# Both triangles of attention keys in one square of 128 columns, with masked values and their differences

## The chip, the cores and the metric

One core of one Trainium2 chip runs the whole program in one launch. The metric is the device time of an execution in microseconds. A core has TensorE (PE; its weight loads appear as PEld), VectorE (DVE), ScalarE (ACT), GpSimd (POOL) and SyncE (SP), each with a queue of its own that is worked off in order; they wait for one another by semaphores. SBUF is the on-chip memory, PSUM the memory of eight banks that TensorE writes to.

## The reference, cut to what matters

A decoder of two layers over 512 tokens of width 1024. Layer 0 is a gated token mixer, layer 1 sliding-window attention over shared keys and values; both have a gated feed-forward part and a gated per-layer embedding. The change lies in the attention of layer 1:

```
def mixer_b(xn, w_q, sinks, w_o, kblk, vblk):
    q = (xn @ w_q).reshape(B, nb, BLOCK, N_KV_HEADS, GQA_GROUP, HEAD_DIM)
    scores = einsum('bnikgd,bnjkd->bnkgij', q, kblk) * (HEAD_DIM ** -0.5)
    i = arange(BLOCK)[:, None];  j = arange(2 * BLOCK)[None, :]
    dist = i + BLOCK - j
    in_band = (dist >= 0) & (dist < WINDOW)
    valid = in_band[None] & ((blk > 0) | (j[None] >= BLOCK))
    scores = scores - slopes * dist
    scores = where(valid, scores, -inf)
    m = maximum(max(scores, axis=-1), sink)
    e = exp(scores - m)
    probs = e / (sum(e, axis=-1) + exp(sink - m))
    out = einsum('bnkgij,bnjkd->bnikgd', probs, vblk)
    return out.reshape(B, S, N_Q_HEADS * HEAD_DIM) @ w_o
```

BLOCK and WINDOW are 128, there are 4 blocks of queries, 16 query heads and 4 key heads; `kblk` and `vblk` hold the previous block and the own one, 256 keys. Of these, a query i of a block sees the own keys j up to i and the previous block's keys j above i: two triangles that together have 128 keys for each query.

## The kernel before

Activations lie with features on the partitions and the 512 tokens along the free dimension. Nearly every matmul operand is split into a high and a low part of type fp32r, and a product is three matmuls: high by high, high by low, low by high (`mm3`, lines 182 to 184; `mm3t`, 193 to 195, with tokens on the output's partitions). Weights come by DMA into a raw tile, ScalarE casts the high part (`wh`, line 155), VectorE subtracts it for the low part (`wl`, line 156), and `pump`, `chunk` and `more` set how far ahead this runs.

Attention goes in 16 steps, four groups (a key head with its four query heads) by four blocks of queries. A step has four functions. `scores(i)`: for each of the four heads two matmuls (lines 702, 703) of the queries with 256 keys (128 in the first block of a group, which has no previous block) into half a PSUM bank; then one VectorE operation (line 705) that adds the table `far` of distances (a huge negative outside the band), scales, takes the minimum with the sink and leaves the row's minimum in `neg`; then ScalarE's exponential with the row's sum in `sm` (line 710), and the sink's own exponential (713, 714). `weights(i)`: sum, reciprocal (720, 721) and the scaling of the four heads, two on VectorE (727), two on ScalarE (725). `turn(i)`: for each block of keys four TensorE transposes of 128x128 into a bank (737) and the split of that bank into a high and a low part by ScalarE and VectorE (240, 241). `mix(i)`: for each block of keys and each pair of heads three matmuls of the values with these (760), then the split of the result into `o2` (766, 767).

The loop over the steps emits `scores(i)`, then what the table `beside` gives for the step (projections of the next group's queries, two of the four value projections `values(c)`, pieces of the output projection `merge`), then `mix(i-2)`, `turn(i-1)` and `weights(i)`. Scores, turn and weights are marked as of high priority, so that the scheduler moves them ahead of the fill on each engine's queue. `values(0)` and `values(1)` are emitted before the loop, `values(2)` and `values(3)` in steps 2 and 3. The queries of a later group pass through `queries` (a scaled copy, a split, four DMAs). Tiles are drawn from pools by tag: `m0` to `m5` (1024 columns), the arena `ah0` to `al8` (512 columns), the two-buffer tags of the pool `tp`. The keys' normalized input `xkv` lies in the arena's slots 0 to 7, which the attention output `o2` takes over.

Of the kernel before, what the change touches and what calls it, by code (L numbers as in the profile page):

```python
# [8 lines left out]
F32 = mybir.dt.float32  # L9
F32R = mybir.dt.float32r  # L10
AF = mybir.ActivationFunctionType
ALU = mybir.AluOpType

P = 128
D = 1024
S = 512
KD = D // P
NC = S // P
# [3 lines left out]
SLOTS = 9  # L22
N = S // 2
HEADS = 16
HD = 64
GROUPS = 4
GQ = HEADS // GROUPS
EPS = 1e-6
FAR = 1e37
# [19 lines left out]
def tile_yoco(ctx: ExitStack, tc: tile.TileContext, t, out: bass.AP, out_b: bass.AP):  # L49
    nc = tc.nc  # L50

    const = ctx.enter_context(tc.tile_pool(name="const", bufs=1))
    hp = ctx.enter_context(tc.tile_pool(name="hp", bufs=1))
    xp = ctx.enter_context(tc.tile_pool(name="xp", bufs=1))
    ap = ctx.enter_context(tc.tile_pool(name="arena", bufs=1))
# [5 lines left out]
    def psum(name):  # L61
        return mmp.tile([P, S], F32, tag="mm", name=name)
# [161 lines left out]
    ps = psum("idle")  # L224
# [14 lines left out]
    def split(src, hi, lo):  # L239
        nc.scalar.copy(hi, src)  # L240
        nc.vector.tensor_sub(lo, src, hi.bitcast(F32))
# [71 lines left out]
    def slope(hd):  # L313
        return 2.0 ** (-8.0 * (hd + 1) / HEADS)
# [145 lines left out]
    for c in range(NC):  # L460
        vps[1].append(psum(f"v1_{c}"))
        mm3t(vps[1][c], xs, parts, 0, S, c)
        if c == 0:
            rt = n0.begin()


    far = const.tile([P, 2 * P], F32, name="far")
    nc.gpsimd.iota(far, pattern=[[1, 2 * P]], base=-P, channel_multiplier=-1,
                   allow_small_or_imprecise_dtypes=True)
    nc.gpsimd.affine_select(out=far, in_=far, pattern=[[-1, 2 * P]], compare_op=ALU.is_ge,  # L470
                            fill=-FAR, base=P, channel_multiplier=1)
    nc.gpsimd.affine_select(out=far, in_=far, pattern=[[1, 2 * P]], compare_op=ALU.is_ge,
                            fill=-FAR, base=-1, channel_multiplier=-1)

    qscale = const.tile([P, KD], F32, name="qscale")
    for hd in range(HEADS):
# [143 lines left out]
        nc.gpsimd.memset(x[:, VW - HD :].bitcast(F32), 0.0)  # L620


    box = {}

    def values(c):
        if c == 0:
            box["v"] = chunk(256, KD)
        ps = psum(f"vv{c}")
        mm3t(ps[:, :256], xkv, box["v"], 0, 256, c)
        pg = ps[:, :256].rearrange("p (g d) -> p g d", g=GROUPS)  # L630
        vh, vl = (x[:, : VW - HD].rearrange("p (c g w) -> p c g w", c=NC, g=GROUPS)[:, c, :, HD:] for x in vt)
        nc.scalar.activation(vh, pg, AF.Copy, scale=rt[:, c : c + 1])
        nc.vector.scalar_tensor_tensor(vl, pg, rt[:, c : c + 1], vh.bitcast(F32),
                                       op0=ALU.mult, op1=ALU.subtract)

    def project(g, j, k0, k1):
        if j == 0 and k0 == 0:
# [17 lines left out]
    def more():  # L655

        pump(state["unit"] + 1)

    beside = {
        -1: [(values, 0), (values, 1)],  # L660
        0: [(project, 1, 0, 0, 8), (more,)],
        1: [(project, 1, 1, 0, 8), (more,)],
        2: [(values, 2), (project, 2, 0, 0, 4)],
        3: [(values, 3), (project, 2, 0, 4, 8), (more,)],
        4: [(project, 2, 1, 0, 4), (more,)],
        5: [(project, 2, 1, 4, 8)],
        6: [(project, 3, 0, 0, 4), (more,)],
# [17 lines left out]
    steps = [(g, n) for g in range(GROUPS) for n in range(NC)]  # L685
    live = {}

    def scores(i):


        g, n = steps[i]
        k0 = 0 if n else P
        nk = 2 * P - k0
        t0 = (n - 1) * P + k0
        pr = mp.tile([P, GQ, 2 * P], F32, tag=f"m{4 + i % 2}", name=f"pr{i}")
        neg = at.tile([P, GQ], F32, tag="neg", bufs=2, name=f"neg{i}")
        for e in range(GQ):
            if e % 2 == 0:
                sc = psum(f"sc{i}_{e}")
            o = sc[:, (e % 2) * 256 : (e % 2) * 256 + nk]  # L700
            q = qs[g][e][:, n * P : (n + 1) * P]
            nc.tensor.matmul(o, q, kh[g // 2][:, g % 2, t0 : t0 + nk], start=True, stop=False)
            nc.tensor.matmul(o, q, kl[g // 2][:, g % 2, t0 : t0 + nk], start=False, stop=True)
            hd = GQ * g + e
            nc.vector.tensor_tensor_reduce(out=pr[:, e, :nk], in0=far[:, k0:], in1=o, scale=-slope(hd),
                                           scalar=nsink[:, hd : hd + 1], op0=ALU.add, op1=ALU.min,
                                           accum_out=neg[:, e : e + 1])
        sm = at.tile([P, GQ], F32, tag="sm", bufs=2, name=f"sm{i}")
        for e in range(GQ):
            nc.scalar.activation(pr[:, e, :nk], pr[:, e, :nk], AF.Exp, bias=neg[:, e : e + 1], scale=-1.0,  # L710
                                 accum_out=sm[:, e : e + 1])
        ds = at.tile([P, GQ], F32, tag="ds", bufs=2, name=f"ds{i}")
        nc.vector.tensor_add(ds, sink[:, GQ * g : GQ * (g + 1)], neg)
        nc.scalar.activation(ds, ds, AF.Exp)
        live[i] = (pr, nk, sm, ds)

    def weights(i):

        pr, nk, sm, ds = live[i]
        nc.vector.tensor_add(ds, ds, sm)  # L720
        nc.vector.reciprocal(ds, ds)
        for e in range(GQ):
            a, r = pr[:, e, :nk], ds[:, e : e + 1]
            if e in (1, 3):
                nc.scalar.activation(a, a, AF.Copy, scale=r)
            else:
                nc.vector.tensor_scalar_mul(a, a, r)
        live[i] = (pr, nk)

    def turn(i):  # L730

        pr, nk = live[i]
        pts = []
        for b in range(nk // P):
            tr = psum(f"tr{i}_{b}")
            for e in range(GQ):
                nc.tensor.transpose(tr[:, e * P : (e + 1) * P], pr[:, e, b * P : (b + 1) * P], ident)
            q = state["pt"] = (state["pt"] + 1) % 3
            if q == 2:
                ph, pl = (ap.tile([P, S], F32R, tag=f"a{x}{SLOTS - 1}", name=f"p{x}{i}_{b}") for x in "hl")  # L740
            else:
                ph, pl = pts4[:, 2 * q, :], pts4[:, 2 * q + 1, :]
            split(tr, ph, pl)
            pts.append((ph, pl))
        live[i] = pts

    def mix(i):
        g, n = steps[i]
        pts = live.pop(i)
        ps = psum(f"pv{i}")[:, : 2 * P]  # L750
        first = True
        for b, halves in enumerate(pts):
            c = n - len(pts) + 1 + b
            ph, pl = (a.rearrange("p (b e t) -> p b e t", b=2, e=2) for a in halves)
            for e in range(2):
                at0 = (c * GROUPS + g) * 2 * HD + (HD if e == 0 else 0)
                vh, vl = (x[:, at0 : at0 + P] for x in vt)
                for lhs, rhs in ((vh, ph), (vh, pl), (vl, ph)):
                    end = b == len(pts) - 1 and e == 1 and lhs is vl
                    nc.tensor.matmul(ps, lhs, rhs[:, :, e, :], start=first, stop=end)  # L760
                    first = False
        cols = slice(n * P, (n + 1) * P)
        for b in range(2):
            oh, ol = o2[2 * g + b]
            src = ps[:, b * P : (b + 1) * P]
            nc.scalar.copy(oh[:, cols], src)
            nc.vector.tensor_sub(ol[:, cols], src, oh[:, cols].bitcast(F32))
# [217 lines left out]
```

## Time and profile before

| | |
|---|---|
| three runs, median (lowest to highest) | 1160.1 us (1159.73 to 1160.7) |
| the profiled execution, its time | 1160.26 us |
| the profiled execution, its span | 1158.2 us |
| TensorE busy | 1145.4 us, 5464 matmuls |
| VectorE busy | 742.0 us |
| ScalarE busy | 529.0 us |
| GpSimd busy | 78.9 us |

The span reaches from the first instruction to the last. Busy time is the time in which at least one instruction of the engine is under way; matmuls overlap, so that a busy TensorE need not be at its best rate. A group of instructions is shown as line, engine, operation, output<-inputs by the program's names, the shapes, the count, then the busy time in us and the mean ns of one, then the idle time of the engine just before them with what ended it. A line in order of time begins with its start and its duration in us.

### The profile page before, as it was taken

The page shows a single profiled execution, that of the slowest core. Times are in us where ns is not written, and L with a number is a line of the kernel's source. Part 1 is how long each engine was busy: PE and PEld are TensorE (multiplying, and loading weights), DVE is VectorE, ACT ScalarE, POOL GpSimd, SP SyncE. Part 2 cuts the span into 40 slices and gives each one's busy share as a digit, 9 for nine tenths or more (in the row PEclk, how much of TensorE's full clock was granted, in tenths as well). Part 3 has the DMA queues.
Part 4 walks back from the last instruction along what each step waited for, and adds up shares of the span by engine and source line. Part 5 has one row for each costly group of instructions (what it writes and reads, how often), then busy time and mean ns, then how long its engine had stood idle before and what let it go on. Part 6 is the DMA issues. An engine that isn't in the chain of part 4 may idle for free.

```text
span 1158.2 us, 13843 instructions
## 1 busy us (share of the span) xinstructions
PE 1145.4 (99%) x5464; PEld 961.9 (83%) x5464; DVE 742.0 (64%) x1165; ACT 529.0 (46%) x860; POOL 78.9 (7%) x87
## 2 busy tenths in 40 slices
PE   9999999999999999999999999999999999999997
PEld 7888888888888888888888888888888888888896
DVE  7356467763676367556877886677636773675665
ACT  6534344431344234544667885544413432344542
POOL 2000310000000000032200002100000000000222
PEclk9999999999999999999999999999999999999999
DMA  9322322323323323233133314232232233224302
GB/s 318 117 82 73 109 76 106 109 73 109 109 64 100 109 91 109 91 109 104 42 92 110 87 43 170 85 109 85 98 109 82 91 100 109 91 88 150 109 1 73
DMA packets 30736, 115.42 MB, mean 100 GB/s; under 512 B 3016, under 2 KB 14928, under 8 KB 21200
## 3 DMA queue, kind: packets, MB, share of 16 engines
q1 hardware_dynamic: 29552, 113.37, 29.1%
q10 hardware_dynamic: 1120, 1.18, 0.3%
q8 instruction: 43, 0.70, 0.3%
q14 instruction: 21, 0.17, 0.0%
HBM read 108.24 MB, written 2.11 MB: 95 GB/s over the span
## 4 chain that ended last, share of the span: by engine, by line
PE 95%; DVE 2%; ACT 1%; issue 1%; DMA 1%; POOL 0%; SPq 0%; POOLq 0%; ACTq 0%
PE up L182 14%; PE up L184 14%; PE up L183 14%; PE d L184 8%; PE d L182 8%; PE d L183 8%; PE gate L182 2%; PE gate L184 2%; PE gate L183 2%; PE pv L760 1%; PE u L182 1%; PE u L183 1%; PE u L184 1%; PE o L182 1%; PE o L183 1%; PE o L184 1%
## 5 line engine op out<-in xcount | busy, mean ns | idle before, releaser
L156 DVE TENSOR_TENSOR wl<-wraw,wh 128x1024 fp32r<-128x1024 f32 (+2 forms) x197 | 239.4, 1216 | 133.5 <-ACT wh L155 132.9
L155 ACT CAST wh<-wraw 128x1024 fp32r<-128x1024 f32 (+1 forms) x196 | 202.1, 1033 | 265.8 <-PE d L183 131.6
L182 PE MATMUL up<-nf00h,wh 128*128 128x512 f32 x352 | 137.2, 390 | 0.0
L182 PE MATMUL up<-nf10h,wh 128*128 128x512 f32 x352 | 137.1, 389 | 0.0
L184 PE MATMUL up<-nf00h,wl 128*128 128x512 f32 x352 | 137.0, 389 | 0.0
L184 PE MATMUL up<-nf10h,wl 128*128 128x512 f32 x352 | 137.0, 389 | 0.0
L183 PE MATMUL up<-nf00l,wh 128*128 128x512 f32 x352 | 136.9, 389 | 0.0
L183 PE MATMUL up<-nf10l,wh 128*128 128x512 f32 x352 | 136.9, 389 | 0.0
L182 PE MATMUL d<-ah,wh 128*128 128x512 f32 x352 | 136.9, 389 | 0.0
L183 PE MATMUL d<-al,wh 128*128 128x512 f32 x352 | 136.9, 389 | 0.0
L184 PE MATMUL d<-ah,wl 128*128 128x512 f32 x352 | 136.9, 389 | 0.0
L351 ACT ACTIVATE c<-hs,vec 128x512 f32<-128x512 f32 x88 | 71.5, 815 | 71.7 <-DVE hs L347 71.1
L352 DVE SCALAR_TENSOR_TENSOR c<-hs,vec,c 128x511 f32<-128x511 f32 x88 | 65.8, 749 | 34.5 <-ACT c L351 34.5
L327 DVE TENSOR_TENSOR h<-h,d 128x512 f32<-128x512 f32 x56 | 38.4, 686 | 73.8 <-PE d L184 73.8
L184 PEld LDWEIGHTS up<-nf00h,wl 128*128 128x128 f32 x352 | 66.1, 188 | 13.9
L183 PEld LDWEIGHTS up<-nf10l,wh 128*128 128x128 f32 x352 | 66.1, 188 | 13.8
L184 PEld LDWEIGHTS up<-nf10h,wl 128*128 128x128 f32 x352 | 66.1, 188 | 13.8
L183 PEld LDWEIGHTS d<-al,wh 128*128 128x128 f32 x352 | 66.1, 188 | 13.8
L240 ACT CAST ah<-a 128x512 fp32r<-128x512 f32 x44 | 27.4, 622 | 109.7 <-DVE a L357 109.6
L184 PEld LDWEIGHTS d<-ah,wl 128*128 128x128 f32 x352 | 66.1, 188 | 13.7
L183 PEld LDWEIGHTS up<-nf00l,wh 128*128 128x128 f32 x352 | 66.1, 188 | 13.6
L182 PEld LDWEIGHTS d<-ah,wh 128*128 128x128 f32 x352 | 66.1, 188 | 13.7
(337 smaller groups left out, 2089.0 us busy)
## 6 DMA issues: line engine op xcount, KB each, us to landing
wraw<-in_w_up SPq DMA_DIRECT2D x44, 1024.0 KB, 4.8
wraw<-in_w_down SPq DMA_DIRECT2D x16, 896.0 KB, 4.6
wraw<-in_w_down SPq DMA_DIRECT2D x8, 1024.0 KB, 4.8
wraw<-in_w_u SPq DMA_DIRECT2D x4, 1024.0 KB, 5.4
wraw<-in_w_out SPq DMA_DIRECT2D x4, 1024.0 KB, 4.8
wraw<-in_w_gate SPq DMA_DIRECT2D x4, 1024.0 KB, 4.8
wraw<-in_w_q SPq DMA_DIRECT2D x4, 1024.0 KB, 5.2
wraw<-in_w_o SPq DMA_DIRECT2D x4, 1024.0 KB, 5.1
```

The lines of the kernel that those rows point to most:

```text
L155: nc.scalar.copy(wh[:, :n], src)
L156: nc.vector.tensor_sub(wl[:, :n], src, wh[:, :n].bitcast(F32))
L182: nc.tensor.matmul(ps, wh[:, a:b], xh, start=st, stop=False)
L183: nc.tensor.matmul(ps, wh[:, a:b], xl, start=False, stop=False)
L184: nc.tensor.matmul(ps, wl[:, a:b], xh, start=False, stop=en)
L240: nc.scalar.copy(hi, src)
L327: nc.vector.tensor_add(h[m], h[m], ps)
L351: nc.scalar.activation(c, hs, AF.Identity, bias=v("conv_b", l * 2 * NJ + col), scale=cw[2])
L352: nc.vector.scalar_tensor_tensor(c[:, 1:], hs[:, : S - 1], cw[1], c[:, 1:], op0=ALU.mult, op1=ALU.add)
L760: nc.tensor.matmul(ps, lhs, rhs[:, :, e, :], start=first, stop=end)
```

## The change

For a step with a previous block the scores of 256 keys are still computed. A predicated copy on VectorE (`copy_predicated`) then writes the own block's scores over the previous block's wherever the key is visible in the own block (mask `own`), so that 128 columns hold both triangles; `far` becomes a square of 128 columns with the distances of both, and `near` serves the first blocks. The reduction, the exponential, the scaling and the transposes then run over 128 columns. The sink is written as a 129th column by GpSimd (`prs[:, :, P]`), so that the exponential's sum includes it, and the separate exponential of the sink and its additions go. Three of the four scalings are ScalarE's.

The weights of both blocks now lie in one transposed square. Its product with the own block's values would give the previous block's triangle the wrong values; so a second, masked copy of the square (zero where the key is an own one: the high part by a VectorE product with the mask `back`, the low part by GpSimd's `affine_select`) is multiplied with the difference of the previous block's values and the own ones. Those differences are made by two further VectorE operations for each of three blocks in `values`, and are split and laid out by GpSimd in `differences`, with zeros between. All four `values` and `differences` come before the loop. The differences take the arena's slots 5 to 7 and the tag `m5`, the two score tiles become one tile `prs` under `m4`. The scores of a bank's two heads are emitted together, with the copy and the reductions after them.

```diff
--- before.py
+++ after.py
@@ -464,13 +464,26 @@
             rt = n0.begin()
 
 
...
+    near = const.tile([P, P], F32, name="near")
+    nc.gpsimd.iota(near, pattern=[[1, P]], base=0, channel_multiplier=-1, allow_small_or_imprecise_dtypes=True)
+    back = const.tile([P, P], F32, name="back")
+    nc.gpsimd.memset(back, -1.0 * P)
+    nc.gpsimd.affine_select(out=back, in_=back, pattern=[[1, P]], compare_op=ALU.is_ge,
+                            fill=0.0, base=-1, channel_multiplier=-1)
+    far = const.tile([P, P], F32, name="far")
+    nc.gpsimd.tensor_add(far, near, back)
+
+    nc.gpsimd.affine_select(out=near, in_=near, pattern=[[-1, P]], compare_op=ALU.is_ge,
+                            fill=-FAR, base=0, channel_multiplier=1)
+
...
 
     qscale = const.tile([P, KD], F32, name="qscale")
     for hd in range(HEADS):
@@ -620,6 +633,31 @@
         nc.gpsimd.memset(x[:, VW - HD :].bitcast(F32), 0.0)
 
 
+    nrt = const.tile([P, NC], F32, name="nrt")
+    nc.vector.tensor_scalar_mul(nrt, rt, -1.0)
+    prs = mp.tile([P, 2, GQ, P + 1], F32, tag="m4", name="prs")
+    EW = ((NC - 1) * 2 + 1) * HD
+    diffs, vdt = [], {}
+
+    def differences():
+
+        for g in range(GROUPS):
+            if g < GROUPS - 1:
+                diffs.append([ap.tile([P, EW], F32R, tag=f"a{x}{5 + g}", name=f"diff{x}{g}") for x in "hl"])
+            else:
+                lastd = mp.tile([P, 2, EW], F32R, tag="m5", name="lastd")
+                diffs.append([lastd[:, 0, :], lastd[:, 1, :]])
+            for x in diffs[g]:
+                nc.gpsimd.memset(x[:, : EW - HD].rearrange("p (b w) -> p b w", w=2 * HD)[:, :, :HD].bitcast(F32), 0.0)
+                nc.gpsimd.memset(x[:, EW - HD :].bitcast(F32), 0.0)
+        for g in range(GROUPS):
+            for c in range(1, NC):
+                dh, dl = (x[:, (2 * c - 1) * HD : 2 * c * HD] for x in diffs[g])
+                src = vdt[c][:, g * HD : (g + 1) * HD]
+                nc.gpsimd.tensor_copy(dh, src)
+                nc.gpsimd.tensor_sub(dl, src, dh.bitcast(F32))
+
+
     box = {}
 
     def values(c):
@@ -632,6 +670,12 @@
         nc.scalar.activation(vh, pg, AF.Copy, scale=rt[:, c : c + 1])
         nc.vector.scalar_tensor_tensor(vl, pg, rt[:, c : c + 1], vh.bitcast(F32),
                                        op0=ALU.mult, op1=ALU.subtract)
+        if c:
+            d = vdt[c] = tp.tile([P, 2 * P], F32, tag="rstd" if c == 3 else "acc", name=f"vd{c}")
+            dg = d.rearrange("p (g d) -> p g d", g=GROUPS)
+            fh, fl = (x[:, : VW - HD].rearrange("p (c g w) -> p c g w", c=NC, g=GROUPS)[:, c - 1, :, HD:] for x in vt)
+            nc.vector.scalar_tensor_tensor(dg, pg, nrt[:, c : c + 1], fh.bitcast(F32), op0=ALU.mult, op1=ALU.add)
+            nc.vector.tensor_add(dg, dg, fl.bitcast(F32))
 
     def project(g, j, k0, k1):
         if j == 0 and k0 == 0:
@@ -657,11 +701,11 @@
         pump(state["unit"] + 1)
 
     beside = {
-        -1: [(values, 0), (values, 1)],
+        -1: [(values, 0), (values, 1), (values, 2), (values, 3), (differences,)],
         0: [(project, 1, 0, 0, 8), (more,)],
         1: [(project, 1, 1, 0, 8), (more,)],
-        2: [(values, 2), (project, 2, 0, 0, 4)],
-        3: [(values, 3), (project, 2, 0, 4, 8), (more,)],
+        2: [(project, 2, 0, 0, 4)],
+        3: [(project, 2, 0, 4, 8), (more,)],
         4: [(project, 2, 1, 0, 4), (more,)],
         5: [(project, 2, 1, 4, 8)],
         6: [(project, 3, 0, 0, 4), (more,)],
@@ -685,80 +729,92 @@
     steps = [(g, n) for g in range(GROUPS) for n in range(NC)]
     live = {}
 
+    def both(x):
+
+        return x.rearrange("p (o k) -> p o k", o=1).to_broadcast([P, 2, P])
+
     def scores(i):
 
 
         g, n = steps[i]
-        k0 = 0 if n else P
-        nk = 2 * P - k0
-        t0 = (n - 1) * P + k0
-        pr = mp.tile([P, GQ, 2 * P], F32, tag=f"m{4 + i % 2}", name=f"pr{i}")
+        nk = 2 * P if n else P
+        t0 = (n - 1) * P if n else 0
+        pr = prs[:, i % 2]
+        nc.gpsimd.tensor_copy(pr[:, :, P], nsink[:, GQ * g : GQ * (g + 1)])
         neg = at.tile([P, GQ], F32, tag="neg", bufs=2, name=f"neg{i}")
-        for e in range(GQ):
-            if e % 2 == 0:
-                sc = psum(f"sc{i}_{e}")
-            o = sc[:, (e % 2) * 256 : (e % 2) * 256 + nk]
-            q = qs[g][e][:, n * P : (n + 1) * P]
-            nc.tensor.matmul(o, q, kh[g // 2][:, g % 2, t0 : t0 + nk], start=True, stop=False)
-            nc.tensor.matmul(o, q, kl[g // 2][:, g % 2, t0 : t0 + nk], start=False, stop=True)
-            hd = GQ * g + e
-            nc.vector.tensor_tensor_reduce(out=pr[:, e, :nk], in0=far[:, k0:], in1=o, scale=-slope(hd),
-                                           scalar=nsink[:, hd : hd + 1], op0=ALU.add, op1=ALU.min,
-                                           accum_out=neg[:, e : e + 1])
+        for b in range(2):
+            sc = psum(f"sc{i}_{b}").rearrange("p (e h k) -> p e h k", e=2, h=2)
+            for j in range(2):
+                o = sc[:, j].rearrange("p h k -> p (h k)")[:, :nk]
+                q = qs[g][2 * b + j][:, n * P : (n + 1) * P]
+                nc.tensor.matmul(o, q, kh[g // 2][:, g % 2, t0 : t0 + nk], start=True, stop=False)
+                nc.tensor.matmul(o, q, kl[g // 2][:, g % 2, t0 : t0 + nk], start=False, stop=True)
+            if n:
+                nc.vector.copy_predicated(sc[:, :, 0, :], both(own.bitcast(mybir.dt.int32)), sc[:, :, 1, :])
+            for j in range(2):
+                e = 2 * b + j
+                hd = GQ * g + e
+                nc.vector.tensor_tensor_reduce(out=pr[:, e, :P], in0=far if n else near, in1=sc[:, j, 0, :],
+                                               scale=-slope(hd), scalar=nsink[:, hd : hd + 1],
+                                               op0=ALU.add, op1=ALU.min, accum_out=neg[:, e : e + 1])
         sm = at.tile([P, GQ], F32, tag="sm", bufs=2, name=f"sm{i}")
         for e in range(GQ):
-            nc.scalar.activation(pr[:, e, :nk], pr[:, e, :nk], AF.Exp, bias=neg[:, e : e + 1], scale=-1.0,
+            nc.scalar.activation(pr[:, e, :], pr[:, e, :], AF.Exp, bias=neg[:, e : e + 1], scale=-1.0,
                                  accum_out=sm[:, e : e + 1])
+        live[i] = (pr, sm)
+
+    def weights(i):
+
+        pr, sm = live[i]
         ds = at.tile([P, GQ], F32, tag="ds", bufs=2, name=f"ds{i}")
-        nc.vector.tensor_add(ds, sink[:, GQ * g : GQ * (g + 1)], neg)
-        nc.scalar.activation(ds, ds, AF.Exp)
-        live[i] = (pr, nk, sm, ds)
-
-    def weights(i):
-
-        pr, nk, sm, ds = live[i]
-        nc.vector.tensor_add(ds, ds, sm)
-        nc.vector.reciprocal(ds, ds)
+        nc.vector.reciprocal(ds, sm)
         for e in range(GQ):
-            a, r = pr[:, e, :nk], ds[:, e : e + 1]
-            if e in (1, 3):
+            a, r = pr[:, e, :P], ds[:, e : e + 1]
+            if e:
                 nc.scalar.activation(a, a, AF.Copy, scale=r)
             else:
                 nc.vector.tensor_scalar_mul(a, a, r)
-        live[i] = (pr, nk)
+        live[i] = pr
+
+    def pair(name):
+        q = state["pt"] = (state["pt"] + 1) % 3
+        if q == 2:
+            return [ap.tile([P, S], F32R, tag=f"a{x}{SLOTS - 1}", name=f"{name}{x}") for x in "hl"]
+        return [pts4[:, 2 * q, :], pts4[:, 2 * q + 1, :]]
 
     def turn(i):
 
-        pr, nk = live[i]
-        pts = []
-        for b in range(nk // P):
-            tr = psum(f"tr{i}_{b}")
-            for e in range(GQ):
-                nc.tensor.transpose(tr[:, e * P : (e + 1) * P], pr[:, e, b * P : (b + 1) * P], ident)
-            q = state["pt"] = (state["pt"] + 1) % 3
-            if q == 2:
-                ph, pl = (ap.tile([P, S], F32R, tag=f"a{x}{SLOTS - 1}", name=f"p{x}{i}_{b}") for x in "hl")
-            else:
-                ph, pl = pts4[:, 2 * q, :], pts4[:, 2 * q + 1, :]
-            split(tr, ph, pl)
-            pts.append((ph, pl))
-        live[i] = pts
+        g, n = steps[i]
+        pr = live[i]
+        tr = psum(f"tr{i}")
+        for e in range(GQ):
+            nc.tensor.transpose(tr[:, e * P : (e + 1) * P], pr[:, e, :P], ident)
+        ph, pl = pair(f"p{i}")
+        split(tr, ph, pl)
+        live[i] = [(ph, pl)]
+        if n:
+            uh, ul = pair(f"u{i}")
+            w = "p (e t) -> p e t"
+            nc.vector.tensor_mul(uh.rearrange(w, e=GQ), tr.rearrange(w, e=GQ),
+                                 back.rearrange("p (o k) -> p o k", o=1).to_broadcast([P, GQ, P]))
+            nc.gpsimd.affine_select(out=ul.rearrange(w, e=GQ), in_=pl.rearrange(w, e=GQ).bitcast(F32),
+                                    pattern=[[0, GQ], [-1, P]], compare_op=ALU.is_ge, fill=0.0, base=-1,
+                                    channel_multiplier=1)
+            live[i].append((uh, ul))
 
     def mix(i):
         g, n = steps[i]
         pts = live.pop(i)
         ps = psum(f"pv{i}")[:, : 2 * P]
-        first = True
+        todo = []
         for b, halves in enumerate(pts):
-            c = n - len(pts) + 1 + b
             ph, pl = (a.rearrange("p (b e t) -> p b e t", b=2, e=2) for a in halves)
             for e in range(2):
-                at0 = (c * GROUPS + g) * 2 * HD + (HD if e == 0 else 0)
-                vh, vl = (x[:, at0 : at0 + P] for x in vt)
-                for lhs, rhs in ((vh, ph), (vh, pl), (vl, ph)):
-                    end = b == len(pts) - 1 and e == 1 and lhs is vl
-                    nc.tensor.matmul(ps, lhs, rhs[:, :, e, :], start=first, stop=end)
-                    first = False
+                at0 = (n - 1 if b else n * GROUPS + g) * 2 * HD + (HD if e == 0 else 0)
+                vh, vl = (x[:, at0 : at0 + P] for x in (diffs[g] if b else vt))
+                todo += [(vh, ph[:, :, e, :]), (vl, ph[:, :, e, :]), (vh, pl[:, :, e, :])]
+        for j, (lhs, rhs) in enumerate(todo):
+            nc.tensor.matmul(ps, lhs, rhs, start=j == 0, stop=j == len(todo) - 1)
         cols = slice(n * P, (n + 1) * P)
         for b in range(2):
             oh, ol = o2[2 * g + b]
```

More of the change, by code (lines that the diff above doesn't have):

```diff
@@ L464, in tile_yoco @@
             rt = n0.begin()
[L467 to L473, printed above, removed]
+    near = const.tile([P, P], F32, name="near")
[8 more added lines that the diff above has]
+                            fill=-FAR, base=0, channel_multiplier=1)
+    own = const.tile([P, P], F32, name="own")
+    nc.gpsimd.memset(own, 1.0)
+    nc.gpsimd.affine_select(out=own, in_=own, pattern=[[-1, P]], compare_op=ALU.is_ge,
+                            fill=0.0, base=0, channel_multiplier=1)
+    nc.gpsimd.memset(back, 1.0)
+    nc.gpsimd.affine_select(out=back, in_=back, pattern=[[-1, P]], compare_op=ALU.is_ge,
+                            fill=0.0, base=-1, channel_multiplier=1)
     qscale = const.tile([P, KD], F32, name="qscale")
```

## The prediction

> **What bounds the kernel now.** I read the page first, then busy time by stretches around the attention stage, then TensorE's instructions in order of time, then the groups of that stage kept apart by shape.
>
> ```profile
> span 1158.2 us, 13843 instructions
> PE 1145.4 (99%) x5464; PEld 961.9 (83%) x5464; DVE 742.0 (64%) x1165; ACT 529.0 (46%) x860; POOL 78.9 (7%) x87
> PE 95%; DVE 2%; ACT 1%; issue 1%; DMA 1%; POOL 0%; SPq 0%; POOLq 0%; ACTq 0%
> ```
>
> TensorE is busy nearly throughout and makes 95% of the chain that ended last: what shortens its own queue shortens the kernel, unless another engine then makes it wait. The change lies in 586 to 706 us; there the picture is closer (columns: stretch, its length, busy time of PE, PEld, DVE, ACT, POOL, granted clock, DMA share, GB/s):
>
> ```profile
> 586.00:625.00 39.00, 38.02 (x244) 33.94 (x242) 29.07 (x80) 27.22 (x68) 0.00 (x0) 1.00 0.36 101
> 625.00:677.00 52.00, 50.83 (x328) 45.29 (x327) 44.77 (x163) 43.52 (x141) 0.00 (x0) 1.00 0.36 102
> 677.00:706.00 29.00, 28.87 (x178) 25.25 (x177) 20.01 (x66) 19.04 (x58) 0.00 (x0) 1.00 0.24 84
> ```
>
> In the middle stretch VectorE is at 44.77 of 52 (86%) and ScalarE at 84%, so a gain on TensorE counts only as far as these two follow. GpSimd has nothing there. The clock is 1.00 and doesn't enter.
>
> **Part 1: TensorE's work.** A busy time can't price a matmul, as they overlap; starts can (TensorE in order of time: start in us, duration, instruction; then a group of the stage: count | busy us, mean ns | idle before it):
>
> ```profile
> 652.77 0.39 PE L183 MATMUL q<-n11l,wh 128*128 128x512 f32 x1
> 653.00 0.39 PE L184 MATMUL q<-n11h,wl 128*128 128x512 f32 x1
> 653.23 0.28 PE L760 MATMUL pv<-ph,vth 128*128 128x256 f32 x1
> 653.34 0.71 PE L737 MATMUL tr<-ident,pr 128*128 128x128 f32 x5
> ...
> 654.25 0.27 PE L737 MATMUL tr<-ident,pr 128*128 128x128 f32 x1
> 654.28 0.36 PE L703 MATMUL sc<-kl,q 128*128 128x256 f32 x1
> ```
> ```profile
> L737 PE MATMUL tr<-ident,pr 128*128 128x128 f32 x112 | 18.3, 273 | 0.0
> ```
>
> A 512-wide matmul follows the one before after 0.23 us, a 256-wide one after 0.11 to 0.12. Five transposes last 0.71, one 0.27, so each further one costs (0.71-0.27)/4 = 0.11. Per step with a previous block (12 of the 16) the change leaves 8 score matmuls of 256 and 12 value matmuls of 256 (two blocks of six before; six with the own values and six with the differences after) and takes 4 of 8 transposes. The four first steps of each group keep their count, and the value projections only move. So 48 transposes go: 48 x 0.11 = **-5.3 us**. From both sides: 0.03 each if the next matmul starts at once behind one (654.25 to 654.28), -1.4; 18.3/112 = 0.163 by busy time, -7.8. I take 0.11, from a closed row of five.
>
> **Part 2: TensorE's waits.** The loss is from start to start, less 0.12 for a 256-wide and 0.11 for a 128-wide matmul (the same view; in brackets the idle time before and who ended it):
>
> ```profile
> 586.68 0.28 PE L193 MATMUL vv<-wh,n10h 128*128 128x256 f32 x1
> ...
> 589.74 0.28 PE L703 MATMUL sc<-kl,q 128*128 128x128 f32 x1
> 590.85 0.33 PE L702 MATMUL sc<-kh,q 128*128 128x128 f32 x1 [0.84 <-DVE q L598]
> ...
> 624.87 0.28 PE L760 MATMUL pv<-pts,vth 128*128 128x256 f32 x1
> 625.53 0.33 PE L702 MATMUL sc<-kh,q 128*128 128x128 f32 x1 [0.38 <-DVE neg L705]
> ...
> 648.50 0.28 PE L760 MATMUL pv<-pts,vth 128*128 128x256 f32 x1
> 649.16 0.33 PE L702 MATMUL sc<-kh,q 128*128 128x128 f32 x1 [0.38 <-DVE neg L705]
> ...
> 671.05 0.28 PE L760 MATMUL pv<-pl,vth 128*128 128x256 f32 x1
> 671.74 0.33 PE L702 MATMUL sc<-kh,q 128*128 128x128 f32 x1 [0.41 <-DVE neg L705]
> ```
>
> The first is 1.0 us: the scores of step 0 stand in TensorE's queue ahead of most of the second value projection, and wait for the queries. With all values ahead, the changed order has 73 of the 96 value matmuls before the first score, 8.7 us from 586.7, to 595.4, when the queries are long there. What pays for it: step 0 starts 4.5 us later (590.85 to 595.4), and steps 2 and 3 lose their 24 value matmuls, 2.8 us of cover each; they are left with 12 projection matmuls, as steps 4 to 9 have now. The two ScalarE copies and two VectorE subtractions that evacuate those values move too, ahead of the reductions of step 1; TensorE has the group-1 projection over them. The other three, 0.54+0.54+0.57 = 1.65 us, are the second head's scores of a bank, which wait until VectorE has read the first head's from the same bank. In the changed order both heads' four matmuls fill a bank in one go, so VectorE is asked for only at a bank's reuse. Together **-2.65 us**. The end without this gain is 0: the waits come back elsewhere.
>
> **Part 3: VectorE and ScalarE**, hidden behind TensorE if they stay below it:
>
> ```profile
> L705 DVE CUSTOM_DVE_ANT_0 pr<-far,sc,nsink 128x256 f32<-128x256 f32 x48 | 21.8, 476 | 1.5 <-PE sc L703 1.2 <-PE tr L737 0.2
> L705 DVE CUSTOM_DVE_ANT_0 pr<-far,sc,nsink 128x128 f32<-128x128 f32 x16 | 5.1, 340 | 0.0
> L241 DVE TENSOR_TENSOR pts<-tr,pts 128x512 fp32r<-128x512 f32 x19 | 13.1, 687 | 3.6 <-ACT pts L240 3.6
> L727 DVE TENSOR_SCALAR pr<-pr,ds 128x256 f32<-128x256 f32 x24 | 7.5, 350 | 0.2
> L727 DVE TENSOR_SCALAR pr<-pr,ds 128x128 f32<-128x128 f32 x8 | 1.9, 284 | 0.1
> L720 DVE TENSOR_TENSOR ds<-ds,sm 128x4 f32<-128x4 f32 x16 | 2.6, 160 | 4.5 <-ACT ds L714 4.4
> L713 DVE TENSOR_TENSOR ds<-sink,neg 128x4 f32<-128x4 f32 x16 | 2.5, 155 | 0.1
> L806 DVE TENSOR_TENSOR z<-gate,np1rstd 128x256 f32<-128x256 f32 x8 | 3.3, 418 | 1.7 <-ACT np1rstd L288 1.2 <-PE gate L184 0.5
> L240 ACT CAST pts<-tr 128x512 fp32r<-128x512 f32 x19 | 11.0, 577 | 3.5 <-PE tr L737 3.0 <-PE pv L760 0.5
> L725 ACT ACTIVATE pr<-pr,ds 128x128 f32<-128x128 f32 x8 | 2.9, 399 | 1.0 <-DVE ds L721 1.0
> ```
>
> VectorE per such step: four reductions fall by 4 x 0.136 = 0.54, two scalings of 256 (0.70) become one of 128 (0.28), the two sink additions (0.32) go; one of two subtractions at 0.69 becomes the masked product of the same shape, taken as equal. Added are two predicated copies of 256 elements within PSUM, which no row shows. The nearest below is a 256-wide operation out of PSUM, 0.42; above, the 512-wide one, 0.69. I take 0.42, as the elements are 256. Sum: -0.54-0.42-0.32+0.84 = -0.44 us a step; at 0.69, +0.10. The differences add two operations near 0.42 for three blocks, once, 2.5 us, under the group-1 projection (24 matmuls, 5.5 us). ScalarE loses a cast (0.58), gains a scaling (0.40) and its exponentials shrink. So both fall about as TensorE does (0.44 a step): **0 on the path**, and without that cover the 24 copies would cost 24 x 0.42 = 10 us.
>
> **Part 4: GpSimd**, new in this stage: a copy of the sink a step, 24 operations and 16 fills for the differences, and a mask over the low half of each transposed block.
>
> ```profile
> L488 POOL TENSOR_SCALAR_AFFINE_SELECT wsT<-wsT 128x1024 f32<-128x1024 f32 x1 | 1.7, 1667 | 19.3 <-DMA wsT<-in_wsT 19.3
> masks.py:199 POOL TENSOR_SCALAR_AFFINE_SELECT ident<-ident 128x128 f32<-128x128 f32 x1 | 0.4, 371 | 0.0
> ```
>
> Between 0.37 and 1.67, half-way in elements, the mask of 512 is an estimate of 0.93 us. The last four value matmuls of a step wait for it, and with them TensorE's queue. From the transposes it takes 0.44 + 0.58 + 0.69 + 0.93 = 2.6 us, with handovers and one copy ahead some 3.5; TensorE has in between the next scores (0.95), the rest of the previous values (1.3), a fill of 9 to 12 matmuls (2.1 to 2.7) and eight value matmuls (0.95): 5.3 to 5.9. Slack 1.8 to 2.4, so nothing, except at the tail, where after the last transposes only 11 value matmuls and the first eight stand (2.3 us): +1.0. The sink copies are queued behind masks of earlier steps, but two steps ahead of their exponential: 0. The first step that uses a difference comes some 15 us after the last value projection; all fills and copies are short: 0, up to +3. One rule speaks against putting this on GpSimd, and the rows come first (GpSimd and VectorE in order of time, then the stage's group):
>
> ```profile
> 543.96 1.34 POOL L270 TENSOR_TENSOR n1acc<-n1acc,n1sq 128x512 f32<-128x512 f32 x1 [4.21 <-ACT n1sq L265]
> ...
> 544.06 2.32 DVE L156 TENSOR_TENSOR wl<-wraw,wh 128x1024 fp32r<-128x1024 f32 x1
> ...
> L156 DVE TENSOR_TENSOR wl<-wraw,wh 128x1024 fp32r<-128x1024 f32 x12 | 14.7, 1222 | 6.0 <-ACT wh L155 6.0
> ```
>
> The weight subtraction takes 1.22 in the attention stage, and 2.32 when it starts 0.10 behind a GpSimd addition: 1.10 lost, down to the addition's end. Twelve of these lie in the stage; with about 20 us of GpSimd work in 110, two or three collide, half a mask each: **+0.5**. The Trainium skill, "SBUF — State Buffer", section "Who interferes with whom", says that VectorE and GpSimd share a port pair as an exclusive lock, taken by VectorE operations with two SBUF inputs; by that rule the trace agrees.
>
> **Sum:** 1158.2 - 5.3 - 2.65 + 1.0 + 0.5 = 1151.7. The profiled execution took 1160.26, 2.06 outside its span, so 1153.8; the runs' median is 1160.1, 0.16 below it: **1153.6 us**.
>
> **The rivals.**
> *VectorE becomes the bound:* the predicated copy costs 0.69. A step is then +0.10 on VectorE, and the stretch 625 to 677 (six of the twelve steps) can't shrink. What remains is 24 transposes (2.6) and the first wait (1.0): 1156.5. For it: 86% and a copy that reads and writes PSUM. Against: TensorE has slack in the fills.
> *The port lock decides:* each of twelve masks delays one VectorE operation by its 0.93, 11.2 us, and half reaches TensorE: -8.0 + 1.0 + 5.6, 1158.7. For it: the 2.32 row. Against: behind the mask's start VectorE mostly has operations out of PSUM.
> *The mask is late (slower):* four matmuls wait on GpSimd at every one of 12 steps. From a wait of 7/12 = 0.58 us a step the gain is gone. At 1.67 for the mask, a 1.22 subtraction ahead of it and 1.2 of VectorE's queue, it comes 3.2 later than reckoned, 1.0 over the slack: 12 us, 1153.6 + 12 = 1165.6. Against: all three would have to meet every step.
> *The transposes were hidden:* TensorE merely waits longer for the exponentials: 1160. Against: 98% busy in the stage.
>
> **How the numbers follow.** Forecast 0.60, VectorE 0.15, lock 0.08, late mask 0.10, hidden 0.07. Low end: transposes at 0.163 and all waits gone, 1160.1-7.8-2.65 = 1149.6, rounded to 1149. The high end takes in all but the late mask: 1160.5. Within 0.2% (1157.8 to 1162.4) can't be told from no change. Faster: forecast, and 0.14 of VectorE's 0.15 and 0.03 of the lock: 0.77; same: 0.12; slower: 0.11.
>
> **What would show it.** Right: 64 transposes, no gap of 1 us before the first scores, none behind the reductions; GpSimd never the releaser of a value matmul but at the end. Wrong: predicated copies near 0.69 with VectorE above 90% in the middle; value matmuls idle behind the mask; transposes idle behind the scalings. A start of the up projection that is not 6 to 7 us earlier refutes the sum.

## The result and the profile after

| | before | after |
|---|---|---|
| median of four runs beside each other (lowest to highest) | 1159.96 us (1159.73 to 1160.7) | 1149.69 us (1149.53 to 1149.89) |
| span of the profiled execution | 1158.2 us | 1147.9 us |

The ratio is 0.9909, with a 95% interval of 0.9898 to 0.9921: 10.3 us less. Forecast were 6.5 us less, 1153.6, with a range of 1149.0 to 1160.5. The time lies in the range, 0.7 us above its low end.

The page of the changed kernel, with span, TensorE's busy time and the shares of the chain that ended last:

```profile
span 1147.9 us, 13840 instructions
PE 1137.0 (99%) x5416; PEld 955.6 (83%) x5416; DVE 736.6 (64%) x1148; ACT 517.1 (45%) x848; POOL 101.4 (9%) x161
...
PE 95%; ACT 1%; DVE 1%; issue 1%; DMA 1%; POOL 0%; SPq 0%; POOLq 0%; ACTq 0%
```

It has 48 matmuls fewer, the transposes counted in Part 1, and the same engine sets the end. Where the 10.3 us came from is seen in the start of the first up projection, the first work behind attention, in TensorE's order of time, before and then after:

```profile
728.33 0.39 PE L182 MATMUL up<-nf10h,wh 128*128 128x512 f32 x1
```
```profile
718.09 0.39 PE L182 MATMUL up<-nf10h,wh 128*128 128x512 f32 x1
```

It starts 10.24 us earlier, so the gain was made by then; 10.10 of it lie in the attention stage itself (table below). The stage by stretches (columns as in the prediction):

```profile
586.00:625.00 39.00, 39.00 (x253) 35.50 (x252) 32.18 (x91) 26.71 (x76) 12.11 (x42) 1.00 0.51 141
625.00:677.00 52.00, 51.88 (x345) 47.24 (x344) 44.87 (x165) 40.59 (x146) 6.64 (x17) 1.00 0.26 72
```

TensorE went from 38.02 to 39.00 of 39 and from 50.83 to 51.88 of 52. VectorE went from 44.77 to 44.87 of 52, 86% both times.

To separate work from waits I added up a plain account over the stage, from the first value matmul to that up projection. Each matmul is entered at the pace at which its kind follows another when nothing waits (0.2275 us for 512 columns, 0.1185 for 256, 0.11 for 128); what is left over of the elapsed time is called excess.

| stage on TensorE | elapsed | at full pace | excess |
|---|---|---|---|
| before (586.68 to 728.33) | 141.65 | 134.94 | 6.71 |
| after (586.54 to 718.09) | 131.55 | 129.66 | 1.89 |

By this account 5.28 us are work and 4.82 are waits. The 5.28 is not measured: it is 48 transposes entered at 0.11, and the waits are what remains (at e4_trans's 0.095 below they would be 4.6 and 5.5). The prediction had 5.3 and, with the costs that it set against them, 2.65 - 1.0 - 0.5 = 1.15.

The waits show in full on the weight loads, and only in part on the matmuls: a matmul still under way covers the time in which the next one's weights stand and wait. The group of weight loads at the head of the scores, before and then after (x64 | busy us, mean ns | idle before them, with what ended it):

```profile
L702 PEld LDWEIGHTS sc<-kh,q 128*128 128x128 f32 x64 | 12.0, 188 | 6.1 <-DVE neg L705 4.1 <-DVE q L598 1.0
```
```profile
L750 PEld LDWEIGHTS sc<-kh,q 128*128 128x128 f32 x64 | 12.2, 190 | 0.3 <-PE sc L751 0.2
```

Of the 6.1 us, 4.1 came in 11 waits for a reduction (`neg`), the longest 0.6, and 1.0 in the one wait for the queries. After, 0.3 is left. Part 2 took only the four gaps that stood out among the matmuls, not this row of before.

What the new operations cost, as groups of the stage:

```profile
L791 PE MATMUL tr<-ident,prs 128*128 128x128 f32 x64 | 12.9, 274 | 0.0
L753 DVE COPY_PREDICATED sc<-own,sc 128x256 f32<-128x256 int32 x24 | 9.9, 423 | 1.5 <-PE sc L751 1.3
L798 DVE TENSOR_TENSOR pts<-tr,back 128x512 fp32r<-128x512 f32 x8 | 5.4, 678 | 0.0
L800 POOL TENSOR_SCALAR_AFFINE_SELECT pts<-pts 128x512 fp32r<-128x512 f32 x4 | 2.5, 634 | 13.6 <-DVE pts L241 13.3 <-PE pv L817 0.3
```

The predicated copy takes 423 ns (taken: 0.42), the masked product 678 (0.69), GpSimd's mask 634 (estimated: 0.93).

### The profile page after: what moved, and what is told of

Same layout as the page of the kernel before. It is cut to its first block, busy times and chain, and to the rows that moved or that the text cites. A ratio compares the mean times of both kernels' runs of the same rounds, so it can differ in the third digit from the quotient of the medians.

```text
span 1147.9 us, 13840 instructions
## 1 busy us (share of the span) xinstructions
PE 1137.0 (99%) x5416; PEld 955.6 (83%) x5416; DVE 736.6 (64%) x1148; ACT 517.1 (45%) x848; POOL 101.4 (9%) x161
## 4 chain that ended last, share of the span: by engine, by line
PE 95%; ACT 1%; DVE 1%; issue 1%; DMA 1%; POOL 0%; SPq 0%; POOLq 0%; ACTq 0%
PE up L183 14%; PE up L182 14%; PE up L184 14%; PE d L183 8%; PE d L182 8%; PE d L184 8%; PE gate L182 2%; PE gate L183 2%; PE gate L184 2%; PE pv L817 1%; PE o L182 1%; PE u L184 1%; PE u L183 1%; PE u L182 1%; PE o L183 1%; PE o L184 1%
## 5 line engine op out<-in xcount | busy, mean ns | idle before, releaser
L182 PEld LDWEIGHTS up<-nf10h,wh 128*128 128x128 f32 x352 | 66.1, 188 | 13.8
L182 PEld LDWEIGHTS up<-nf00h,wh 128*128 128x128 f32 x352 | 66.1, 188 | 13.7
```

The lines of the kernel that those rows point to most:

```text
L182: nc.tensor.matmul(ps, wh[:, a:b], xh, start=st, stop=False)
```

## The experiments

The question after the result: is the larger gain the order of scores and values (theory), or a lighter VectorE and ScalarE (rival)? Then each term of the sum by itself. The kernel before, measured beside each run, took 1160.34 to 1160.41 us, 0.4 more than beside the changed kernel; a difference to the changed kernel's 1149.69 below may thus be too large by that 0.4. The elapsed time of the stage, read as in the table above from the one profiled execution of each run, doesn't depend on that:

| run | e1 | e2 | e3 | e9 | e4 | e5 | e6 | e7 | e8 | e10 |
|---|---|---|---|---|---|---|---|---|---|---|
| compared with | before | before | before | before | after | after | after | after | after | after |
| stage, us | -3.5 | -1.4 | -4.5 | -1.8 | +4.6 | +1.3 | +0.3 | +0.9 | +3.5 | +4.1 |

**e1_order: the kernel before, with a bank's two heads emitted together.**

```diff
+        for b in range(2):
+            sc = psum(f"sc{i}_{b}")
+            for j in range(2):
...
+                nc.tensor.matmul(o, q, kh[...], start=True, stop=False)
+                nc.tensor.matmul(o, q, kl[...], start=False, stop=True)
+            for j in range(2):
...
+                nc.vector.tensor_tensor_reduce(...)
```

> The kernel before with one edit: the four score matmuls of a bank's two heads are emitted together, then their two reductions (still 256 wide). Of the 10.1 us that the attention stage lost with the change, 5.3 are taken as the 48 transposes and 4.8 as waits of TensorE. Theory A (the waits came from the order of the scores in a bank): 1.7 to 3.5 us faster than before, about 1157. Theory B (they went because VectorE and ScalarE have less to do at 128 columns): within 0.5 us of before, 1160.

1156.15 against 1160.34 us, ratio 0.9962 (0.9947 to 0.9977): -4.2. Its weight loads:

```profile
L702 PEld LDWEIGHTS sc<-kh,q 128*128 128x128 f32 x64 | 12.2, 190 | 2.1 <-DVE q L598 1.2 <-DVE pts L241 0.6 <-DVE pl L241 0.2
```

All waits for `neg` are gone, 4.1 us of them, and the time fell by about as much (4.2 by the medians, 3.5 by the stage), more than the theory's 1.7 to 3.5 by the medians. Only 0.8 came back elsewhere.

**e2_values: the kernel before, with all four values ahead.**

```diff
-        -1: [(values, 0), (values, 1)],
+        -1: [(values, 0), (values, 1), (values, 2), (values, 3)],
...
-        2: [(values, 2), (project, 2, 0, 0, 4)],
-        3: [(values, 3), (project, 2, 0, 4, 8), (more,)],
+        2: [(project, 2, 0, 0, 4)],
+        3: [(project, 2, 0, 4, 8), (more,)],
```

> The kernel before with one edit: all four value projections ahead of the steps. Theory A (the first scores no longer wait for the queries): 1.0 to 1.3 us faster, about 1158.9. Rival (steps 2 and 3 lose 24 value matmuls of cover each, and the waits come back there): no gain, 1160, or up to 2 us slower.

1158.51 us, 0.9984 (0.9974 to 0.9994): -1.8.

```profile
L702 PEld LDWEIGHTS sc<-kh,q 128*128 128x128 f32 x64 | 12.1, 188 | 4.7 <-DVE neg L705 3.7
```

The gain is above the 1.0 to 1.3 expected. The wait for the queries (1.0) is gone, and those for `neg` fell a little. Steps 2 and 3, which lost 2.8 us of cover each, did not pay for it.

**e3_both: the two together.**

> The kernel before with both edits. Theory A: the two add up, 2.7 to 4.8 us faster, 1155.2 to 1157.3; at 4.8 nothing is left for the lighter VectorE and ScalarE. Theory B: at most 1.3 us faster, 1158.7 or more.

1155.30 us, 0.9956 (0.9941 to 0.9971): -5.0, against 6.0 of the two runs added (by the stage 4.5 against 5.0); with intervals of 1.7 us to either side that is no difference. The up projection starts at 723.52, 4.8 earlier than before, and the excess is 2.17.

```profile
L702 PEld LDWEIGHTS sc<-kh,q 128*128 128x128 f32 x64 | 12.2, 190 | 1.0 <-DVE pts L241 0.6 <-DVE pl L241 0.2
```

About half of the change's gain thus needs neither square nor mask.

**e4_trans: the changed kernel, with the 48 transposes put back.** Each step with a previous block makes its four transposes twice into the same bank.

```diff
-        for e in range(GQ):
+        for e in [*range(GQ)] * (2 if n else 1):
             nc.tensor.transpose(tr[:, e * P : (e + 1) * P], pr[:, e, :P], ident)
```

> The changed kernel with its four transposes of every step with a previous block done twice into the same bank, so 48 transposes are back and nothing else. Forecast's price of 0.11 us each: 5.3 us slower than the changed kernel, 1155.0. Price 0.03: 1151.1. Price 0.163: 1157.5. If TensorE has slack by now: 1149.7.

1154.38 us, 0.9947 (0.9932 to 0.9962): 4.7 over the changed kernel by the medians, 4.6 by the stage's elapsed time (136.13 against 131.55).

```profile
L791 PE MATMUL tr<-ident,prs 128*128 128x128 f32 x112 | 20.6, 275 | 0.0
```

48 transposes are worth 4.6/48 = 0.095 us each. The excess at 0.11 is 1.19 here against 1.89 in the changed kernel, so they may as well cost 0.11 and cover 0.7 us of other waits; the run can't tell these apart. The rival that they were hidden has fallen.

**e5_copy2: the changed kernel, with each predicated copy made twice.**

```diff
-            if n:
+            for _ in range(2 if n else 0):
                 nc.vector.copy_predicated(sc[:, :, 0, :], ..., sc[:, :, 1, :])
```

> The changed kernel with every predicated copy done twice (24 more operations of 0.42 us, 10 us of VectorE). If VectorE's work is hidden by TensorE, as the forecast has it: at most 1.5 us slower, 1149.7 to 1151.2. If VectorE is close to being the bound (86% in the middle stretch): half of the 10 us or more shows, 1154.7 or later.

1151.58 us, 0.9925 (0.991 to 0.9939): 1.9 over the changed kernel. VectorE got 24 x 0.42 = 10 us of operations more; as neighbouring ones overlap, its busy time on the page rose by 6.7 us (736.6 to 743.3):

```profile
L753 DVE COPY_PREDICATED sc<-own,sc 128x256 f32<-128x256 int32 x48 | 19.4, 424 | 1.8 <-PE sc L751 1.5
```
```profile
625.00:677.00 52.00, 51.77 (x336) 46.20 (x334) 47.83 (x174) 40.22 (x143) 7.00 (x17) 1.00 0.30 80
```

Even at 47.83 of 52 (92%) at least seven tenths of these 6.7 us stay behind TensorE. VectorE doesn't bound the changed kernel.

**e6_mask2: the changed kernel, with GpSimd's mask applied twice, one behind the other.**

```diff
-            nc.gpsimd.affine_select(out=ul..., in_=pl..., ...)
+            for x in (pl, ul):
+                nc.gpsimd.affine_select(out=ul..., in_=x..., ...)
```

> The changed kernel with GpSimd's mask of the low half done twice in a row (12 more of 0.63 us). If the mask has some 2 us of slack, as the forecast has it: at most 0.7 us slower, at the tail, 1149.7 to 1150.4. If the value matmuls wait for it step by step: 12 x 0.63, 7.6 us slower, 1157.3.

1149.76 us, 0.9908 (0.9892 to 0.9925): 0.1 over the changed kernel. TensorE's waits for GpSimd in the stage (waited for: us in total, times, longest):

```profile
PEld pv L818 <- POOL pts L801: 0.4, 1, 0.4
```

One value matmul of the last step waits, 0.4 us; none of the other eleven steps does. A mask 0.64 us later costs nothing there, so the slack there is more than that.

**e7_maskv: the changed kernel, with that mask as a second VectorE product.**

```diff
-            nc.gpsimd.affine_select(out=ul..., in_=pl..., ...)
+            nc.vector.tensor_mul(ul..., pl..., back...)
```

> The changed kernel with the mask of the low half on VectorE (a product with the mask table, 12 of about 0.69 us) in place of GpSimd. If GpSimd's latency and its collisions with VectorE cost little: same or up to 1.5 us slower, 1149.7 to 1151.2. If the collisions cost what was forecast (0.5) and the tail waits for GpSimd: up to 0.7 us faster, 1149.0.

1150.68 us, 0.9917 (0.9902 to 0.9932): 1.0 over the changed kernel, with 12 x 0.685 = 8.2 us of operations more on VectorE (6.1 of busy time). If GpSimd's mask had delayed VectorE by several us, taking it away would have shown; a delay of the forecast 0.5 would not, as the added products may cost as much as e5_copy2's copies did.

**e9_banks: the kernel before, with a bank of its own for each head.** This asks whether it is the shared bank or the order that made the waits.

```diff
-            if e % 2 == 0:
-                sc = psum(f"sc{i}_{e}")
-            o = sc[:, (e % 2) * 256 : (e % 2) * 256 + nk]
+            sc = psum(f"sc{i}_{e}")
+            o = sc[:, :nk]
```

> The kernel before with one edit: each head's scores get a PSUM bank of their own, in the old order of matmuls and reductions (four banks a step in place of two). If the waits come from two heads sharing a bank (the second head's scores wait for the first head's reduction): as fast as the kernel with the scores emitted together, 3 to 4 us faster than before. If it is the order itself that counts, or if eight banks are too few for four a step: no gain, or slower.

1158.27 against 1160.41 us, 0.998 (0.997 to 0.999): -2.1, half of e1_order's.

```profile
L701 PEld LDWEIGHTS sc<-kh,q 128*128 128x128 f32 x64 | 12.1, 190 | 4.2 <-DVE pts L241 1.2 <-DVE q L598 1.2 <-PE sc L702 0.9
```

The waits for `neg` fell from 4.1 to 0.3 (by the waits of TensorE's loads): they were those of a shared bank. But twice the banks are drawn from the same eight, and waits for the split of the transposes (1.2), which reads a bank, and for TensorE itself (0.9) took part of their place. The order gains twice as much, as it needs no further bank.

**e8_byhead: the changed kernel, head by head as before,** each with a predicated copy of 128 columns.

```diff
-            if n:
-                nc.vector.copy_predicated(sc[:, :, 0, :], both(own...), sc[:, :, 1, :])
-            for j in range(2):
+                if n:
+                    nc.vector.copy_predicated(sc[:, j, 0, :], own..., sc[:, j, 1, :])
```

> The changed kernel with the old order head by head: two score matmuls, a predicated copy of 128 columns, the reduction (48 copies of 128 in place of 24 of 256). If the bank's sharing made the waits before, they come back, longer by the copy: 3 to 6 us slower than the changed kernel, 1152.7 to 1155.7. If the square of 128 columns with its lighter work is what removed them: at most 1 us slower.

1153.05 us, 0.9936 (0.9921 to 0.9951): 3.4 over the changed kernel.

```profile
L750 PEld LDWEIGHTS sc<-kh,q 128*128 128x128 f32 x64 | 12.1, 189 | 4.4 <-issue 1.6 <-DVE neg L756 1.6
```

The bank's waits are back, 1.6 us in six, and one pause of 1.6 ahead of step 4's scores, whose queries then came late by DMA. Two things moved at once, as 48 copies at 290 ns also take more of VectorE than 24 at 423; so this run agrees with e1_order but doesn't price the order by itself.

**e10_fill: an attempt to beat the changed kernel,** with the projections of groups 2 and 3 spread one step later and the pieces of the output projection gathered in steps 11 to 13, so that late steps have more cover.

```diff
-        2: [(project, 2, 0, 0, 4)],
-        3: [(project, 2, 0, 4, 8), (more,)],
+        2: [(project, 2, 0, 0, 3)],
+        3: [(project, 2, 0, 3, 6), (more,)],
...
-        9: [(project, 3, 1, 4, 8)],
+        9: [(project, 3, 1, 0, 4)],
+        10: [(project, 3, 1, 4, 8), (more,)],
```

> The changed kernel with the projections of groups 2 and 3 spread one step later, so that steps 2 to 5 have 9 matmuls beside them in place of 12 and steps 10 to 13 have 12 in place of 6 to 9. The stage's waits that are left (1.9 us) lie after step 9. If they come from too little fill there: up to 1.5 us faster, 1148.2 to 1149.5. If the early steps then wait instead: same or slower.

1153.48 us, 0.9939 (0.9925 to 0.9954): 3.8 slower than the changed kernel, where up to 1.5 faster was hoped for. TensorE in order of time, at the first step of group 3:

```profile
662.62 0.28 PE L817 MATMUL pv<-u9l,diffh 128*128 128x256 f32 x1
665.32 0.30 PE L750 MATMUL sc<-kh,q 128*128 128x128 f32 x1 [2.42 <-DMA q<-qf]
...
668.08 0.63 PE L183 MATMUL o<-ol,wh 128*128 128x512 f32 x1
668.51 0.63 PE L184 MATMUL o<-oh,wl 128*128 128x512 f32 x1
```

The scores wait 2.42 us for queries that still travel by DMA: the projection was too late for its four transfers. What came after the wait stands in the last section. No version here beats the changed kernel.

## Why the prediction came out as it did

**Part 1, the transposes, held.** 5.3 us were predicted, at 0.11 each; e4_trans gives 4.6, at 0.095. A row of five transposes, start to end, priced them within a sixth, and neither bound (0.03, 0.163) was near.

**Part 2, the waits, is the term that was mis-sized.** Its mechanisms were right, as e1_order and e2_values show one by one, its size was not: "Together -2.65 us", from one wait for the queries and three for a bank. e3_both, which makes these two edits alone, gained 5.0 us by the medians and 4.5 by the stage. The three largest bank waits were counted and the other eight were not, since a matmul's idle time shows a wait only when it outlasts the matmul ahead of it: 0.28 us from start to end, against 0.12 from start to start. The weight loads' row has all eleven. Its cautious lower end, that the waits come back elsewhere, happened only in part: 0.8 us in e1_order.

**Part 3 held.** The copy took 0.42 as chosen. VectorE's share of the middle did not move from 86%, and what e5_copy2 added stayed covered for the most part. That rules out *VectorE becomes the bound*. The full price without cover was put at 10 us; with the cover there is, doubling the copies cost 1.9.

**Part 4 was too dear.** The mask took 0.634 instead of 0.93 us, and the +1.0 at the tail didn't come. The last mask in GpSimd's order of time, and TensorE's last value matmuls:

```profile
689.49 0.63 POOL L800 TENSOR_SCALAR_AFFINE_SELECT pts<-pts 128x512 fp32r<-128x512 f32 x1 [6.54 <-DVE pts L241]
```
```profile
687.32 0.60 PE L791 MATMUL tr<-ident,prs 128*128 128x128 f32 x4
...
690.20 0.87 PE L817 MATMUL pv<-pts,lastd 128*128 128x256 f32 x6
```

From the transposes' end (687.92) to the mask's (690.12) are 2.2 us, not 3.5, and TensorE had other matmuls to do up to 690.20. e6_mask2 then lengthened the chain and met just this wait, 0.4 us. The +0.5 was for masks that meet a weight subtraction; none of the twelve did. GpSimd's other new work ran beside a weight subtraction twice from 602 to 605 us, where the differences are made (each engine in order of time):

```profile
600.72 0.58 POOL L657 CAST diffh<-vd 128x64 fp32r<-128x64 f32 x3
...
602.10 1.81 POOL L657 CAST diffh<-vd 128x64 fp32r<-128x64 f32 x3
603.87 1.58 POOL L658 TENSOR_TENSOR diffl<-vd,diffh 128x64 fp32r<-128x64 f32 x2
```
```profile
602.17 1.24 DVE L156 TENSOR_TENSOR wl<-wraw,wh 128x1024 fp32r<-128x1024 f32 x1
...
603.95 1.32 DVE L156 TENSOR_TENSOR wl<-wraw,wh 128x1024 fp32r<-128x1024 f32 x1
```

The subtractions took 1.24 and 1.32 against 1.22 alone; here GpSimd's small operations were stretched, three casts from 0.58 to 1.81, and nothing on TensorE waits for them. What masks did meet were two of VectorE's scalings, which took 0.67 and 0.60 instead of 0.28 (last section), 0.7 us in all; no weight load of the changed kernel's stage is listed as waiting for VectorE. So *the port lock decides* is out: it would have needed 11.2 us of delay on VectorE. *The mask is late* is out by e6_mask2 and its one wait, *the transposes were hidden* by e4_trans.

**The sum, put right:** from the runs alone, the two edits of e3_both are 4.5 us by the stage and the 48 transposes of e4_trans 4.6: 1158.2 - 4.5 - 4.6 = 1149.1 us of span, against 1147.9 measured. (The account's 5.28 and 4.82 close the sum better, but only because its second term is what the first leaves over.) The prediction's own test, an up projection "6 to 7 us earlier", failed at 10.24, and with it the sum, by 3.8 us between its 1151.7 and the span measured. The waits left out (4.5 - 2.65 = 1.9), the two costs that didn't come (1.5) and the gain that stays open (1.0) make 4.4 in the same sense; the transposes, taken 0.7 too dear, go against them. Its other signs of being right came: 64 transposes, no wait for a reduction left, GpSimd nowhere the releaser of a value matmul. That the time still lay in the range is luck: the low end was set by other means, the transposes at 0.163, which e4_trans refutes.

**What stays open:** e3_both's 4.5 and e4_trans's 4.6 leave 1.0 of the stage's 10.1 us unexplained. It may be the shorter reductions and scalings, which let steps hand over sooner; but the intervals of these runs reach 1.7 us to either side, and nothing here isolates it. The changed kernel with its values back in steps 2 and 3 wasn't tried, as the differences need them all.

## What to carry to other kernels

Read the idle time of the weight loads as well as that of the matmuls: a short wait hides behind a matmul under way, and eleven such waits were worth nearly as much here as 48 transposes. Where two results share a PSUM bank, issue all matmuls of the bank ahead of its first reader; here that cost no bank and no matmul. When a large edit brings a reordering with it, try the reordering alone, as it may hold half of the gain.

## What the runs showed of the hardware

In e10_fill the granted clock fell soon after a TensorE idle time of 2.42 us (windows of 4 us, columns as above):

```profile
662.00:666.00 4.00, 1.58 (x12) 1.36 (x11) 2.72 (x11) 2.96 (x14) 0.77 (x2) 1.00 0.73 219
666.00:670.00 4.00, 4.00 (x14) 3.21 (x13) 1.09 (x6) 0.88 (x4) 0.19 (x1) 0.59 0.02 4
670.00:674.00 4.00, 4.00 (x30) 3.77 (x30) 2.89 (x5) 2.68 (x6) 0.57 (x1) 0.98 0.00 0
```

The window behind the wait has a clock of 0.59 (in windows of 1 us it is 0.86, then 0.50 three times, so it fell some 1.4 us after TensorE had resumed), and its 512-wide matmuls start 0.43 us apart (668.08 to 668.51) instead of 0.23; seven of them so, which makes 7 x 0.2 = 1.4 us on top of the wait. The pause of 1.46 us in e8_byhead left the clock at 1.00; no run has a pause between the two lengths. The Trainium skill, "TensorE: Matmul & The Clock Gate", section "Part 1: The HAM clock gate (the "warmup" mystery)", has the clock fall to half after an idle window of about 3.4 us; the size agrees with the pace measured, the length doesn't, as the gap here was shorter by 1.0 us. A new wait can thus cost more than its own length: here the stage grew by 4.1 us.

The other surprise is who gives way. In the kernel before, a VectorE subtraction lost 1.10 us to a GpSimd addition of 512 columns under way. Beside the changed kernel's GpSimd operations of 64 columns it lost 0.02 and 0.10, and GpSimd's casts lost 1.23. The order of the starts fits all of this: the subtraction that lost 1.10 started 0.10 behind the addition, while the cast that lost most started at 602.27, 0.10 behind the subtraction (602.17 to 603.41), and ended 0.10 behind it. It fits the two scalings as well, each started just behind a mask (0.04 us in this pair, the row of GpSimd and then that of VectorE):

```profile
663.95 0.63 POOL L800 TENSOR_SCALAR_AFFINE_SELECT pts<-pts 128x512 fp32r<-128x512 f32 x1 [0.34 <-PE pv L817]
```
```profile
663.99 0.67 DVE L776 TENSOR_SCALAR prs<-prs,ds 128x128 f32<-128x128 f32 x1
```

The scaling ended 0.08 behind the mask. VectorE's reductions, which read PSUM, lost nothing: 15 that ran beside a mask took 0.34 us, as the 49 others did. No run here varies the width or the order by itself.
